# Out projection issued in code order, with next weights split inside the last column tile; adaLN-side weight pairs loaded two K tiles ahead

## The chip, the cores and the metric

The kernel runs on one core of one Trainium2 chip. The metric is the device time of one execution in microseconds (us). The core has a matrix engine (TensorE, PE in the rows; its weight loads are PEld), VectorE (DVE), ScalarE (ACT), GpSimd (POOL) and SyncE (SP). In this kernel every DMA is issued by SP, from one queue, in order. An issue can wait for a semaphore, and then everything behind it on SP waits too.

## The reference, cut to what matters

One layer of a hybrid decoder on 2048 prompt tokens and 8 single-token samples, model width 2048, all in fp32:

```python
shift, scale, gate = split(silu(c) @ w_c + b_c, 3)          # adaLN
h    = rmsnorm(x, g_pre) * (1 + scale) + shift
proj = h @ w_in                                             # u_a, v_a, z_a, x_b, z_b
y_a  = u_a * mix(layernorm(v_a)) * silu(z_a)                # gated MLP, chunks of 128 tokens
y_b  = glu(S5(x_b)) * silu(z_b)                             # diagonal state space model
o    = concat(y_a, y_b) @ w_out
out  = x + gate * rmsnorm(o, g_post)
```

## The kernel before, in words

**Precision.** Each fp32 factor is split in two rounded parts, hi and lo, and each product is three matmuls: hi by hi, hi by lo, lo by hi (`mm3`, L97 to L99). A weight tile comes by DMA as a raw tile `wraw` of 128x1024 (0.524 MB, L108); its two halves ("pieces") are split by ACT (`whi`, L90) and then by DVE or POOL (`wlo`, L85). `lo_engs` says which engine makes the lo of the next piece: DVE and POOL in turn, and in block 3 and behind it DVE, DVE, DVE, POOL. Each tag of split weights has 5 buffers (NW), the raw tiles have 3.

**Startup.** It is written in manual order. SP loads the 16 x tiles, small constants, and the adaLN weights (`wraw<-in_wss`, 64 tiles, 8 in flight). DVE builds a small selector `sel` from the identity (L230, L232) and adds up the squares of x (L342). Then a loop over 16 K tiles multiplies 6 column tiles of w_in with h while it makes the adaLN vectors that the next K tile needs: 4 matmul groups `ada` (L275), a copy `t<-ada` by DVE (L279), a selection `adat` by PE (L286), and a scale of x. The weights of the 6 column tiles come as three pairs (`wraw<-in_win`, tag wraw2, 2 buffers), one set for each group of 4 K tiles; before, a pair is asked for in the first two K tiles of the group that uses it.

**Middle.** Input projection, gated MLP and S5 of four blocks of 512 tokens (phase 1). Tile's scheduler orders these by its own cost estimates. In the S5 part small matrices are copied out of PSUM, `sc` and half of `kf` by DVE.

**Out projection.** `phase3(b)` does 512 tokens of block b (blocks 0 to 2): first a K loop over 16 K tiles with 4 column tiles side by side, then the column tiles n = 4 to 15 one after the other, each with 16 K tiles of 3 matmuls. Block 3 has 264 tokens in this form and 6 tiles side by side. `phase3_rows` does the last 256 tokens the other way round: y is stationary, 32 weight tiles (`wraw<-in_woutr`, called W(i) here) of 2 pieces each feed 12 matmuls each, W(i+4) is asked for while step i runs.

**Finish.** The output of a block is finished in 16 steps while the next block (for block 3, the rows stage) multiplies. The generator `final` loads the residual `xres`, makes the rms factor `oR`, and in each step n:

```python
            V.tensor_mul(o, o, R[:, 0:nn])
            (V if n % 2 else G).tensor_tensor(o, o, x, op=ALU.add)
            SP.dma_start(self.O["yT"][...], o)
            yield 1
```

These are L1154, L1155 and L1156 (with L1145 the load of `xres`); in the changed kernel they are L1156, L1157, L1158 and L1147. `finish_some(n)` takes n steps. O(n) below is the output DMA of step n. In the kernel before, Tile's scheduler also orders all of the out projection: what stands in the code is not the order on an engine.

Of the kernel before, what the change touches and what calls it, by code (L numbers as in the profile page):

```python
# [11 lines left out]
F32 = mybir.dt.float32  # L12
# [11 lines left out]
NB = 4  # L24
# [3 lines left out]
G = 64  # L28
GC = 16
P = 64  # L30
KT = D // 128
# [11 lines left out]
NHL = 32  # L43
NT = 6
NW = 5
OB = 20
LAG = 6
NR_ = 8
XR0 = 41
# [13 lines left out]
class Builder:  # L63
# [155 lines left out]
    def constants1(self):  # L219
        c = self.cp  # L220
        def load(name, shape):
            t = c.tile(shape, F32, name="c_" + name)
            self.SP.dma_start(t, self.I[name])
            return t
        self.ident = load("ident", [128, 128])
        self.bcT = load("bcT", [128, 48])
        self.gpre = load("gpre", [128, KT])
        self.gpost = load("gpost", [128, KT])
        self.sel = c.tile([128, 9], F32, name="sel")
        self.V.tensor_add(self.sel, self.ident[:, 0:9], self.ident[:, 32:41])  # L230
        for i in (64, 96):
            self.V.tensor_add(self.sel, self.sel, self.ident[:, i : i + 9])  # L232

    def constants2(self):
        I, SP, V, S, T = self.I, self.SP, self.V, self.S, self.T
# [510 lines left out]
    def s5_mats(self, pp, i):  # L746


        V, SP, I, T, G, S = self.V, self.SP, self.I, self.T, self.G, self.S
        X = G  # L750
        NQ = 2
# [4 lines left out]
        b = tl([128, 2, NQ, GC], "sb", 2)  # L756
# [39 lines left out]
                k = (ri * NQ + q) * 32  # L796
                T.matmul(pc[:, k : k + 32], cp[:, q, ri, :], wg[:, q, :], start=True, stop=True)
        c = tl([128, 2, NQ, 32], "sc")
        V.tensor_copy(c.rearrange("p r q c -> p (r q c)"), pc[:, 0 : 2 * NQ * 32])
        dw = tl([32, NQ, 32], "dw")  # L800
        mul(dw, wg, dc[:, :, None].to_broadcast([32, NQ, 32]))
        yield
# [47 lines left out]
                T.matmul(pk[g * 32 : g * 32 + 32, 0:128], bd[:, ri, q].rearrange("p g c -> p (g c)"),  # L850
                         Fm[:, ri, q, jh * 4 : jh * 4 + 4, :].rearrange("p j c -> p (j c)"), start=ri == 0, stop=ri == 1)
        for g, q, jh in quarters:
            (S.copy if jh else V.tensor_copy)(kf[:, q, jh * 4 : jh * 4 + 4, :].rearrange("p j c -> p (j c)"), pk[g * 32 : g * 32 + 32, 0:128])
# [238 lines left out]
    def phase3(self, b, ws, y):  # L1092

        V, G, SP = self.V, self.G, self.SP
        rs = ranges(b) if b < NB - 1 else ranges(b)[1:]
        c0 = rs[0][0]
        nn = rs[-1][0] + rs[-1][1] - c0
        ng = 4 if b < NB - 1 else 6
        ssq = self.xp.tile([128, TB + ND], F32, tag="ssq", bufs=2, name=self.nm("ossq"))
        kw = [{}, self.wkw]  # L1100
        ws = ws or [self.wgroup(0, 0, ng, *kw)]
        acc = [[self.ps.tile([128, 512], F32, tag="acc" if g < 4 else "aux", bufs=4, name=self.nm("acc"))] for g in range(ng)]
        os_ = []
        for k in range(KT):
            while len(y) < min(KT, k + 6):
                y.append(self.yload(b, len(y)))
            if k in (11, 13, 15):
                self.finish_some(1)
            if k % 4 == 0 and k < KT - 4:
                ws.append(self.wgroup(0, k // 4 + 1, ng, *(kw[::-1] if k // 4 % 2 == 0 else kw)))  # L1110
            for g in range(ng):
                self.kstep(acc[g], ws[k // 4][g], k, y[k], rs, k == 0, k == KT - 1)
        ynext = []
        w = self.wcol(self.I["wout"][ng])
        for g in range(ng):
            self.finish_some(1)
            os_.append(self.ev_o(b, g, acc[g], rs, ssq, G))
        for n in range(ng, 16):
            ac = [self.ps.tile([128, 512], F32, tag="acc", bufs=4, name=self.nm("acc")) for _ in rs]
            nxt = []  # L1120
            for k in range(KT):
                if k % 8 == 0 and n < 15:
                    nxt += self.wsplit(self.whalf(self.I["wout"][n + 1], k // 8), **(self.wkw if k else {}))
                self.kstep(ac, w, k, y[k], rs, k == 0, k == KT - 1)
                if k == 13:
                    self.run_later()
                if n == 15 and b < NB - 1 and k >= 4 and k % 2 == 0:
                    ynext.append(self.yload(b + 1, len(ynext)))
            self.finish_some(1 if n < 15 or b == NB - 1 else 16)
            if b == NB - 1 and n % 2 == 0 and 6 <= n < 14:  # L1130
                self.gg_rows((n - 6) // 2)
            os_.append(self.ev_o(b, n, ac, rs, ssq, G))
            w = nxt
        self.finish_some(16)
        self.finish = self.final(ssq, nn, os_, b * TB + c0, b * TB)
        return y if b == NB - 1 else ynext

    def final(self, ssq, nn, os_, t0, out0):

# [19 lines left out]
    def gg_rows(self, f):  # L1159

        dg = self.tile_()[:, 0:512]
        for j in range(4):
            self.S.activation(dg[:, j * 128 : j * 128 + 128], self.ident, AF.Identity, scale=self.GG[:, f * 4 + j, 0:1])
        def turn():
            po = self.ps.tile([128, 512], F32, tag="aux", bufs=4, name=self.nm("ggr"))
            self.T.matmul(po, self.ones, dg, start=True, stop=True)
            t = self.tile_()[:, 0:512]
            self.S.copy(t, po)
            self.ggr.append(t)
        self.later.append(turn)  # L1170

    def phase3_rows(self, b, y):
# [3 lines left out]
        src = lambda i: self.I["woutr"][i // 8][:, i % 8 * 2 : i % 8 * 2 + 2, :].rearrange("p k m -> p (k m)")  # L1176
        kws = [{}, self.wkw]
        ws = {i: self.wsplit(src(i), **kws[i % 2]) for i in range(4)}
        os_, xs = {}, {}
        mm = T.matmul  # L1180
        def final(c):
# [18 lines left out]
        for f in range(4):  # L1200
# [3 lines left out]
            for k in range(KT + lag):  # L1204
# [19 lines left out]
                            final(c)  # L1224
                if k < KT and k % 2:
                    if i + 4 < 32:
                        ws[i + 4] = self.wsplit(src(i + 4), **kws[i % 2])
# [9 lines left out]
    def startup(self, st, NG, ntl):  # L1237
# [6 lines left out]
                raws[i] = self.wraw(I["wss"][i // 4][:, i % 4 * 4 : i % 4 * 4 + 4, :].rearrange("p k m -> p (k m)"), st, "sraw", NR_)  # L1244
        ws = [[] for _ in range(NG)]
        def wraw(g, kq):
            pair[g, kq] = self.wraw(self.wpair(I["win"], ntl[1][g], kq), st, "wraw2", 2)
        def wsplit(g, kq):
            a, b = self.wpieces(pair.pop((g, kq)), pool=st, tags=("swh", "swl"), bufs=NG + 2, engs=(V, G))
            ws[g].append(a)  # L1250
# [2 lines left out]
        self.constants1()  # L1253
        for i in range(NR_):
            raw(i)
        wraw(0, 0)
        wraw(2, 0)
        ssq = self.tile_()
        for k in range(KT):
            self.stat_add(st, xs[k], ssq, k, TB, V)  # L1260
        R = self.R[0]
        def ada(ps, i):
            self.ada_mm(ps, raws.pop(i), i % 4)
            raw(i + NR_)
# [8 lines left out]
        sb = self.ada_copy(ps)  # L1273
        self.hscale(xs[0], R, 0)
        wsplit(0, 0)
        wraw(4, 0)
        self.ada_ss2(0, sb)
        self.h = [self.hmake(xs[0], 0, 0)]
        wsplit(2, 0)
# [7 lines left out]
        for s in range(2, KT + 2):  # L1287
# [6 lines left out]
            for q in range(NG):  # L1294
# [11 lines left out]
                if q == 2 and prev is not None:  # L1306
                    self.h.append(self.hmake(xs[s - 1], 0, s - 1))
                if s < KT:
                    if s % 4 == 0 and q in (0, 2):
                        wraw(q, s // 4)  # L1310
                    if s % 4 == 1 and q == 3:
                        wraw(4, s // 4)
                    if (s % 4, q) in ((0, 3), (1, 2), (1, 4)):
                        wsplit(0 if q == 3 else q, s // 4)
            if s == KT:
# [4 lines left out]
    def build(self):  # L1320
# [127 lines left out]
        cm_x, self.xp = self.pool("x3")  # L1448
        self.finish = None
        self.wkw = {"pool": self.xp, "tags": ("w3h", "w3l"), "bufs": 5}  # L1450
        for b in range(NB):
            if b == NB - 1:
                self.lo_engs = [V, V, V, G]
                self.ggr = []
            y = self.phase3(b, [ws0] if b == 0 else None, y0 if b == 0 else y)
        self.phase3_rows(NB - 1, y)
        self.close(cm_x)
        for cm in reversed(cms[1:]):
            self.close(cm)
# [71 lines left out]
```

## Time and profile before

| what | value |
|---|---|
| time, median of 3 runs | 2974.43 us (2973.07 to 2980.24) |
| the profiled execution | 2969.24 us |
| its span, first to last instruction | 2967.4 us |
| PE busy | 2846.7 us, 96% of the span |
| DVE, ACT, POOL busy | 1590.0, 1059.7, 1046.0 us |
| mean granted TensorE clock | 0.987 of full speed |
| moved by DMA | 581.14 MB, 196 GB/s over the span |

PE has work nearly all of the time, so the time is the sum of the matmuls and of the places where PE stops. A matmul counts as busy until its modelled end; the number of matmuls in a stretch says more than the busy share. A queue of SP is written SPq. A row of a timeline gives the start, the length, the engine, the line and the operation, and in brackets how long the engine had been idle before it and what ended that.

### The profile page before, as it was taken

To read this page: it belongs to the slowest core of one execution; us is meant where nothing else is said; L and a number is where in the kernel's file an instruction comes from. 1 tells how busy PE (TensorE), PEld (TensorE's weight loads), DVE (VectorE), ACT (ScalarE), POOL (GpSimd) and SP (SyncE) were. 2 spreads that over 40 slices of the span, in tenths; PEclk is the share of its full clock that TensorE was granted. 3 is DMA by queue.
4 is the path that set the end of the run, shared out by engine and by line. 5 is a ranking of instruction groups with operands and counts; after the bars stand their busy time and mean duration, and the time that the engine had idled before them with its cause. 6 is when DMAs were issued, how large, how long until landed. Compare 5 with 4: busy or idle time off the path is not lost.

```text
span 2967.4 us, 44344 instructions
## 1 busy us (share of the span) xinstructions
PE 2846.7 (96%) x15804; PEld 2387.4 (80%) x15804; DVE 1590.0 (54%) x3026; ACT 1059.7 (36%) x1960; POOL 1046.0 (35%) x971
## 2 busy tenths in 40 slices
PE   5899899999999999999999999999999999999896
PEld 3567677777999999988888888888888878878785
DVE  4347946648543646466546745583641361543755
ACT  3224433433333232333334332433243423434442
POOL 0107735364242232323232223222324353352433
PEclk9999999999999999999999999999999999999998
DMA  8777898997887373856576566646573463564666
GB/s 299 270 201 217 237 258 236 258 270 221 194 205 214 105 232 119 251 163 189 166 215 195 161 193 185 209 132 215 162 217 110 117 206 121 142 213 128 202 199 206
DMA packets 456560, 581.14 MB, mean 196 GB/s; under 512 B 216594, under 2 KB 303122, under 8 KB 456338
## 3 DMA queue, kind: packets, MB, share of 16 engines
q1 hardware_dynamic: 456338, 578.32, 65.3%
q8 instruction: 124, 2.03, 0.3%
q14 instruction: 98, 0.79, 0.1%
HBM read 466.87 MB, written 102.66 MB: 192 GB/s over the span
## 4 chain that ended last, share of the span: by engine, by line
PE 57%; DVE 8%; DMA 3%; issue 2%; ACT 1%; SPq 0%; POOL 0%; DVEq 0%; ACTq 0%; POOLq 0%
PE acc L99 17%; PE acc L97 16%; PE acc L98 16%; DVE Ub L898 2%; DVE o L1154 1%; DVE wlo L85 1%; DMA x<-in_xT 1%; DMA wraw<-in_wout 1%; PE mix L530 1%; PE acc L1214 1%; PE acc L1215 1%; PE acc L1216 1%; DMA wraw<-in_woutr 1%; PE pg L979 1%; DVE sct L908 1%
## 5 line engine op out<-in xcount | busy, mean ns | idle before, releaser
L97 PE MATMUL acc<-hi,whi 128*128 128x512 f32 (+2 forms) x3200 | 1131.4, 355 | 4.0 <-DVE x L374 2.2
L98 PE MATMUL acc<-lo,whi 128*128 128x512 f32 (+2 forms) x3200 | 1122.3, 351 | 2.4 <-DVE lo L85 2.1
L99 PE MATMUL acc<-hi,wlo 128*128 128x512 f32 (+2 forms) x3200 | 1122.0, 351 | 1.9 <-DVE wlo L85 1.6
L85 DVE TENSOR_TENSOR wlo<-wraw,whi 128x512 fp32r<-128x512 f32 x628 | 518.9, 835 | 882.4 <-ACT whi L90 858.5
L90 ACT CAST whi<-wraw 128x512 fp32r<-128x512 f32 x960 | 581.4, 621 | 1142.7 <-PE acc L98 791.0
L85 POOL TENSOR_TENSOR wlo<-wraw,whi 128x512 fp32r<-128x512 f32 x332 | 459.8, 1387 | 1131.8 <-ACT whi L90 1027.3
L97 PEld LDWEIGHTS acc<-hi,whi 128*128 128x128 f32 x3200 | 603.2, 189 | 100.7 <-issue 23.4
L99 PEld LDWEIGHTS acc<-hi,wlo 128*128 128x128 f32 x3200 | 603.6, 189 | 90.7 <-DVE wlo L85 4.7
L98 PEld LDWEIGHTS acc<-lo,whi 128*128 128x128 f32 x3200 | 604.6, 189 | 80.2 <-DVE lo L85 3.9
L99 PE MATMUL acc<-yhi,wlo 128*128 128x512 f32 (+1 forms) x1024 | 379.6, 372 | 16.7 <-DVE wlo L85 15.2
L97 PE MATMUL acc<-yhi,whi 128*128 128x512 f32 (+1 forms) x1024 | 378.6, 370 | 6.4 <-ACT whi L90 3.6
L98 PE MATMUL acc<-ylo,whi 128*128 128x512 f32 (+1 forms) x1024 | 378.3, 370 | 0.0
L99 PEld LDWEIGHTS acc<-yhi,wlo 128*128 128x128 f32 x1024 | 195.3, 191 | 54.5 <-DVE wlo L85 18.0
L97 PEld LDWEIGHTS acc<-yhi,whi 128*128 128x128 f32 x1024 | 195.6, 191 | 42.5 <-ACT whi L90 4.1
L98 PEld LDWEIGHTS acc<-ylo,whi 128*128 128x128 f32 x1024 | 195.4, 191 | 34.0
L898 DVE SCALAR_TENSOR_TENSOR Ub<-Ub,apow 128x128 f32<-128x128 f32 (+6 forms) x384 | 143.3, 440 | 2.5 <-ACT Ub L885 2.2
L987 POOL TENSOR_TENSOR sg<-sg,zbl 128x264 f32<-128x264 f32 x64 | 54.7, 855 | 191.6 <-DVE sg L986 127.8
L1076 POOL TENSOR_TENSOR ossq<-ossq,osq 128x512 f32<-128x512 f32 (+1 forms) x60 | 81.8, 1363 | 47.8 <-ACT osq L1069 47.0
L369 ACT ACTIVATE hi<-x,shiftT 128x512 fp32r<-128x512 f32 x96 | 68.4, 724 | 82.1 <-DVE x L368 78.8
L368 DVE SCALAR_TENSOR_TENSOR x<-x,GT,R 128x512 f32<-128x512 f32 x96 | 82.2, 872 | 23.9 <-DMA x<-in_xT 23.7
L90 ACT CAST hh<-hr 128x264 fp32r<-128x264 f32 x64 | 26.4, 414 | 191.4 <-DMA hr<-Ub 107.3
L342 POOL TENSOR_TENSOR ssq<-ssq,t 128x512 f32<-128x512 f32 (+1 forms) x45 | 60.9, 1353 | 72.7 <-ACT t L341 71.8
(287 smaller groups left out, 2798.5 us busy)
## 6 DMA issues: line engine op xcount, KB each, us to landing
wraw<-in_win SPq DMA_DIRECT2D x320, 512.0 KB
wraw<-in_wout SPq DMA_DIRECT2D x128, 512.0 KB
xr<-XB SPq DMA_DIRECT2D x128, 272.0 KB
x<-in_xT SPq DMA_DIRECT2D x128, 256.0 KB
wraw<-in_wss SPq DMA_DIRECT2D x64, 512.0 KB
XB<-t SPq DMA_DIRECT2D x64, 256.0 KB
wraw<-in_wgt SPq DMA_DIRECT2D x32, 512.0 KB
MQ<-qh SPq DMA_DIRECT2D x128, 128.0 KB
```

The lines of the kernel that those rows point to most:

```text
L85: eng.tensor_tensor(out, a, b, op=ALU.subtract)
L90: self.S.copy(hi, raw)
L97: mm(acc, whi, xhi, start=start, stop=False)
L98: mm(acc, whi, xlo, start=False, stop=False)
L99: mm(acc, wlo, xhi, start=False, stop=stop)
L342: add_eng.tensor_tensor(ssq[:, 0:n], ssq[:, 0:n], sq[:, 0:n], op=ALU.add)
L368: V.scalar_tensor_tensor(xt, xt, self.GT[:, k, 0:1], R[:, 0:TB], op0=ALU.mult, op1=ALU.mult)
L369: S.activation(hi[:, 0:TB], xt, AF.Identity, bias=self.shiftT[:, k, 0:1])
L530: T.matmul(pm[:, c * 128 : c * 128 + 128], self.vtok[:, c, hs], self.wsT[:, h, :], start=True, stop=True)
L898: V.scalar_tensor_tensor(o, i, f, o, op0=ALU.mult, op1=ALU.add)
L987: self.G.tensor_tensor(sg, sg, zb, op=ALU.mult)
L1076: eng.tensor_tensor(ssq[:, 0:nn], ssq[:, 0:nn], sq[:, 0:nn], op=ALU.add)
```

## The change

- `phase3` for all blocks and `phase3_rows` stand in one `with tc.manual_schedule()`: each engine gets these instructions in the order of the code.
- In the last column tile (n = 15) the first weight pairs of the next block (or the first two W of the rows stage) are loaded and split between the K steps. The finish steps of the K loop stand behind the matmuls of K tiles 11, 13 and 15 and not ahead of them.
- Startup: wraw2 has 3 buffers; the third first pair is asked for with the first two; a group's pairs are asked for in the third K tile of the group before it. The adds that build `sel` stand behind the adds of the squares.
- S5: the copies `sc` and `kf` go from DVE to ACT.
- Buffers: 19 tiles for o and not 20; the broadcast gate rows `ggr` have a tag of their own.

```diff
-        self.sel = c.tile([128, 9], F32, name="sel")          # constants1, ahead of the squares
-        self.V.tensor_add(self.sel, self.ident[:, 0:9], self.ident[:, 32:41])
...
-        V.tensor_copy(c.rearrange("p r q c -> p (r q c)"), pc[:, 0 : 2 * NQ * 32])
+        S.copy(c.rearrange("p r q c -> p (r q c)"), pc[:, 0 : 2 * NQ * 32])
...
-            (S.copy if jh else V.tensor_copy)(kf[:, q, jh * 4 : jh * 4 + 4, :]...)
+            S.copy(kf[:, q, jh * 4 : jh * 4 + 4, :]...)
...                                                             # phase3, K loop
-            if k in (11, 13, 15):
-                self.finish_some(1)
             if k % 4 == 0 and k < KT - 4:
                 ws.append(self.wgroup(0, k // 4 + 1, ng, ...))
             for g in range(ng):
                 self.kstep(acc[g], ws[k // 4][g], k, y[k], rs, k == 0, k == KT - 1)
+            if k in (11, 13, 15):
+                self.finish_some(1)
...                                                             # phase3, column tiles
-                if n == 15 and b < NB - 1 and k >= 4 and k % 2 == 0:
-                    ynext.append(self.yload(b + 1, len(ynext)))
+                if n == 15 and b < NB - 1:
+                    if k >= 4 and k % 2 == 0:
+                        ynext.append(self.yload(b + 1, len(ynext)))
+                    if k in (1, 9) or (k == 13 and b == NB - 2):
+                        g = len(wnext)
+                        wnext.extend(self.wsplit(self.wpair(self.I["wout"], g, 0), **kw[g // 4]))
+                elif n == 15 and k in (1, 9):
+                    wnext.append(self.rows_w(len(wnext)))
...                                                             # startup
-            pair[g, kq] = self.wraw(self.wpair(I["win"], ntl[1][g], kq), st, "wraw2", 2)
+            pair[g, kq] = self.wraw(self.wpair(I["win"], ntl[1][g], kq), st, "wraw2", 3)
...
-        wraw(0, 0)
-        wraw(2, 0)
+        for g in (0, 2, 4):
+            wraw(g, 0)
         ssq = self.tile_()
         for k in range(KT):
             self.stat_add(st, xs[k], ssq, k, TB, V)
         R = self.R[0]
+        self.sel = self.cp.tile([128, 9], F32, name="sel")
+        V.tensor_add(self.sel, self.ident[:, 0:9], self.ident[:, 32:41])
...
-                    if s % 4 == 0 and q in (0, 2):
-                        wraw(q, s // 4)
-                    if s % 4 == 1 and q == 3:
-                        wraw(4, s // 4)
+                    if s % 4 == 2 and s < KT - 4 and q % 2 == 0:
+                        wraw(q, s // 4 + 1)
...                                                             # build
-        for b in range(NB):
-            ...
-            y = self.phase3(b, [ws0] if b == 0 else None, y0 if b == 0 else y)
-        self.phase3_rows(NB - 1, y)
+        with tc.manual_schedule():
+            for b in range(NB - 1):
+                y, ws = self.phase3(b, ws, y)
+            self.lo_engs = [V, V, V, G]
+            self.ggr = []
+            y, ws = self.phase3(NB - 1, ws, y)
+            self.phase3_rows(NB - 1, y, ws)
```

**Startup, SP.** Before, at the beginning of the loop: the adaLN tiles (`in_wss`) run on, and a pair (`in_win`) comes two K tiles later, apart from the next.

```order
L108 DMA wraw_448<-in_wss 128x1024
L108 DMA wraw_454<-in_wss 128x1024
L108 DMA wraw_474<-in_wss 128x1024
L108 DMA wraw_480<-in_wss 128x1024
L108 DMA wraw_504<-in_wss 128x1024
L108 DMA wraw_510<-in_wss 128x1024
L108 DMA wraw_530<-in_wss 128x1024
L108 DMA wraw_536<-in_wss 128x1024
L108 DMA wraw_545<-in_win 128x2x512
```

The same stretch in the changed kernel:

```order
L108 DMA wraw_433<-in_win 128x2x512
L108 DMA wraw_450<-in_wss 128x1024
L108 DMA wraw_456<-in_wss 128x1024
L108 DMA wraw_463<-in_win 128x2x512
L108 DMA wraw_471<-in_win 128x2x512
L108 DMA wraw_480<-in_wss 128x1024
```

The three pairs of the second group stand ahead of 8, 8 and 12 adaLN tiles that they stood behind.

**From block 0 to block 1, SP.** Before: four weight tiles of 128x1024, for the column tiles 4 and 5 of block 1, stand ahead of the first output O(0) of block 0.

```order
L108 DMA wraw_23840<-in_wout 128x1024
L108 DMA wraw_23850<-in_wout 128x1024
L108 DMA wraw_23899<-in_wout 128x1024
L108 DMA wraw_23933<-in_wout 128x1024
L1047 DMA t_24769<-YA_0_97 128x512
L1047 DMA t_24781<-YA_1_98 128x512
L1047 DMA t_24793<-YA_2_99 128x512
L1047 DMA t_24805<-YA_3_100 128x512
L1047 DMA t_24817<-YA_4_101 128x512
L1047 DMA t_24829<-YA_5_102 128x512
L1156 DMA out_yT<-o_22538 128x512
```

The changed kernel:

```order
L1158 DMA out_yT<-o_22540 128x512
L1147 DMA xres_23808<-in_xT 128x512
L1158 DMA out_yT<-o_22543 128x512
L1147 DMA xres_23837<-in_xT 128x512
L1158 DMA out_yT<-o_22548 128x512
L108 DMA wraw_23842<-in_wout 128x1024
L108 DMA wraw_23852<-in_wout 128x1024
L1147 DMA xres_23862<-in_xT 128x512
L1158 DMA out_yT<-o_22553 128x512
```

The weights of column tile 4 stand behind O(0), O(1) and O(2); those of tile 5 stand further down, behind O(6).

**Rows stage, SP and DVE.** Before, SP, the last of 19 W in a row and the first outputs of block 3 behind them:

```order
L108 DMA wraw_28022<-in_woutr 128x1024
L108 DMA wraw_28049<-in_woutr 128x1024
L108 DMA wraw_28076<-in_woutr 128x1024
L1156 DMA out_yT<-o_26789 128x264
L1145 DMA xres_27895<-in_xT 128x264
L1145 DMA xres_27924<-in_xT 128x264
L1156 DMA out_yT<-o_26808 128x264
L1156 DMA out_yT<-o_26789 128x264
```

The changed kernel, SP, the same outputs (W(11) is `wraw_27916`):

```order
L1147 DMA xres_27897<-in_xT 128x264
L1158 DMA out_yT<-o_26791 128x264
L108 DMA wraw_27916<-in_woutr 128x1024
L1147 DMA xres_27926<-in_xT 128x264
L1158 DMA out_yT<-o_26810 128x264
L108 DMA wraw_27943<-in_woutr 128x1024
L1147 DMA xres_27953<-in_xT 128x264
L1158 DMA out_yT<-o_26810 128x264
L108 DMA wraw_27970<-in_woutr 128x1024
```

And DVE there:

```order
L85 TENSOR_TENSOR wlo_27923<-wraw_27916,whi_27922 128x512
L1156 TENSOR_TENSOR o_26810<-o_26810,oR_27834 128x264
L85 TENSOR_TENSOR wlo_27950<-wraw_27943,whi_27949 128x512
L1156 TENSOR_TENSOR o_26810<-o_26810,oR_27834 128x264
L1157 TENSOR_TENSOR o_26810<-o_26810,xres_27862 128x264
L85 TENSOR_TENSOR wlo_27973<-wraw_27970,whi_27972 128x512
L85 TENSOR_TENSOR wlo_27977<-wraw_27970,whi_27976 128x512
L1156 TENSOR_TENSOR o_26831<-o_26831,oR_27834 128x264
```

SP has one W between two outputs, and so on for all 16 outputs; DVE has the lo of that W ahead of the multiplication for the next output. (In block 3 two column tiles share one buffer `o_...`, so each name comes twice.)

## Rows read from the trace of the kernel before

**Rows 1.** Waits of PE, 0 to 240 us: total, times, longest.

```profile
PE adat L286 <- DVE t L279: 20.9, 7, 6.3
```

**Rows 2.** Timeline of the startup loop, 71 to 83 us.

```profile
71.42 0.38 SPq L108 DMA_DIRECT2D wraw<-in_win  x1
...
80.38 0.62 ACT L90 CAST whi<-wraw 128x512 fp32r<-128x512 f32 x1 [7.46 <-DMA wraw<-in_win]
...
82.12 1.02 PE L286 MATMUL adat<-sel,t 128*128 128x9 f32 x4 [6.35 <-DVE t L279]
```

**Rows 3.** Timeline of PE: four of the 15 adat in the loop.

```profile
46.34 0.61 PE L286 MATMUL adat<-sel,t 128*128 128x9 f32 x4 [2.35 <-DVE t L279]
...
91.34 0.51 PE L286 MATMUL adat<-sel,t 128*128 128x9 f32 x4
98.36 0.51 PE L286 MATMUL adat<-sel,t 128*128 128x9 f32 x4
...
172.34 0.51 PE L286 MATMUL adat<-sel,t 128*128 128x9 f32 x4
```

**Rows 4.** Windows: length, busy (count) by engine, PEclk, DMA share, GB/s.

```profile
100.00:110.00 10.00, 10.00 (x78) 6.17 (x67) 4.71 (x8) 4.42 (x8) 1.50 (x2) 1.00 1.02 373
117.40:124.20 6.80, 6.42 (x28) 4.02 (x29) 2.70 (x5) 1.44 (x2) 1.13 (x1) 0.50 0.27 75
2300.00:2400.00 100.00, 100.00 (x433) 81.02 (x432) 37.15 (x44) 39.10 (x60) 29.73 (x22) 1.00 0.42 123
2820.00:2840.00 20.00, 18.99 (x153) 18.79 (x154) 12.16 (x17) 11.90 (x25) 7.93 (x7) 1.00 0.74 236
```

**Rows 5.** Timeline of DVE and ACT before the loop.

```profile
15.87 0.17 DVE L230 TENSOR_TENSOR sel<-c_ident 128x9 f32<-128x9 f32 x1 [11.24 <-DMA c_ident<-in_ident]
...
16.36 11.82 DVE L342 TENSOR_TENSOR t<-t,t 128x512 f32<-128x512 f32 x15
...
29.13 0.62 ACT L90 CAST whi<-wraw 128x512 fp32r<-128x512 f32 x1 [3.46 <-DMA wraw<-in_win]
```

**Rows 6.** Waits of PE, 2150 us to the end.

```profile
PE acc L99 <- DVE wlo L85: 15.2, 5, 5.3
```

**Rows 7.** Waits of SP's queue, 2180 us to the end.

```profile
SPq L108 <- DVE wlo L85: 413.8, 120, 9.5
...
SPq L1156 <- POOL o L1155: 19.1, 14, 4.7
```

**Rows 8.** Timeline of DVE, POOL and PE between block 1 and block 2.

```profile
2391.50 0.69 DVE L160 TENSOR_SCALAR t<-ssum 128x512 f32<-128x512 f32 x1 [7.88 <-PE ssum L159]
...
2401.04 19.02 DVE L1154 TENSOR_TENSOR o<-o,oR 128x512 f32<-128x512 f32 x15
...
2401.81 1.68 POOL L1155 TENSOR_TENSOR o<-o,xres 128x512 f32<-128x512 f32 x1 [8.56 <-DVE o L1154]
...
2421.32 0.74 PE L99 MATMUL acc<-yhi,wlo 128*128 128x512 f32 x1 [4.57 <-DVE wlo L85]
```

**Rows 9.** Timeline of the rows stage.

```profile
2854.20 0.33 SPq L108 DMA_DIRECT2D wraw<-in_woutr  x1
...
2857.75 1.14 ACT L90 CAST whi<-wraw 128x512 fp32r<-128x512 f32 x2 [1.47 <-DMA wraw<-in_woutr]
2858.41 1.29 DVE L85 TENSOR_TENSOR wlo<-wraw,whi 128x512 fp32r<-128x512 f32 x2 [1.36 <-ACT whi L90]
...
2861.91 1.36 DVE L85 TENSOR_TENSOR wlo<-wraw,whi 128x512 fp32r<-128x512 f32 x1 [2.21 <-ACT whi L90]
...
2894.65 1.86 POOL L1155 TENSOR_TENSOR o<-o,xres 128x264 f32<-128x264 f32 x2
2898.44 0.42 DVE L1155 TENSOR_TENSOR o<-o,xres 128x264 f32<-128x264 f32 x1
...
2909.31 0.38 SPq L108 DMA_DIRECT2D wraw<-in_woutr  x1
...
2915.42 0.80 PE L1214 MATMUL acc<-whi,yhi 128*128 128x512 f32 x1 [8.42 <-ACT whi L90]
```

More of the change, by code (lines that the diff above doesn't have):

```diff
@@ L45 @@
 NW = 5
-OB = 20
+OB = 19
 LAG = 6
@@ L228, in constants1 @@
         self.gpost = load("gpost", [128, KT])
-        self.sel = c.tile([128, 9], F32, name="sel")
-        self.V.tensor_add(self.sel, self.ident[:, 0:9], self.ident[:, 32:41])
-        for i in (64, 96):
-            self.V.tensor_add(self.sel, self.sel, self.ident[:, i : i + 9])
     def constants2(self):
@@ L852, in s5_mats @@
         for g, q, jh in quarters:
-            (S.copy if jh else V.tensor_copy)(kf[:, q, jh * 4 : jh * 4 + 4, :].rearrange("p j c -> p (j c)"), pk[g * 32 : g * 32 + 32, 0:128])
+            S.copy(kf[:, q, jh * 4 : jh * 4 + 4, :].rearrange("p j c -> p (j c)"), pk[g * 32 : g * 32 + 32, 0:128])
         V.tensor_add(kf[:, :, 0, :], kf[:, :, 0, :], dw)
@@ L1100, in phase3 @@
         kw = [{}, self.wkw]
-        ws = ws or [self.wgroup(0, 0, ng, *kw)]
+        ws = [ws]
         acc = [[self.ps.tile([128, 512], F32, tag="acc" if g < 4 else "aux", bufs=4, name=self.nm("acc"))] for g in range(ng)]
@@ L1112, in phase3 @@
                 self.kstep(acc[g], ws[k // 4][g], k, y[k], rs, k == 0, k == KT - 1)
-        ynext = []
+            if k in (11, 13, 15):
+                self.finish_some(1)
+        ynext, wnext = [], []
         w = self.wcol(self.I["wout"][ng])
@@ L1135, in phase3 @@
         self.finish = self.final(ssq, nn, os_, b * TB + c0, b * TB)
-        return y if b == NB - 1 else ynext
+        return (y if b == NB - 1 else ynext), wnext
     def final(self, ssq, nn, os_, t0, out0):
@@ L1166, in turn @@
             self.T.matmul(po, self.ones, dg, start=True, stop=True)
-            t = self.tile_()[:, 0:512]
+            t = self.xp.tile([128, 512], F32, tag="ggr", bufs=4, name=self.nm("ggt"))
             self.S.copy(t, po)
@@ L1170, in gg_rows, with rows_w, phase3_rows @@
         self.later.append(turn)
-    def phase3_rows(self, b, y):
+    def rows_w(self, i):
+        return self.wsplit(self.I["woutr"][i // 8][:, i % 8 * 2 : i % 8 * 2 + 2, :].rearrange("p k m -> p (k m)"), **(self.wkw if i % 2 else {}))
+    def phase3_rows(self, b, y, ws):
         V, G, S, T, SP = self.V, self.G, self.S, self.T, self.SP
         ssq = self.sp_.tile([128, 2, 4], F32, name="ssqr")
-        src = lambda i: self.I["woutr"][i // 8][:, i % 8 * 2 : i % 8 * 2 + 2, :].rearrange("p k m -> p (k m)")
-        kws = [{}, self.wkw]
-        ws = {i: self.wsplit(src(i), **kws[i % 2]) for i in range(4)}
+        ws = dict(enumerate(ws))
+        for i in range(len(ws), 4):
+            ws[i] = self.rows_w(i)
         os_, xs = {}, {}
@@ L1226, in phase3_rows @@
                     if i + 4 < 32:
-                        ws[i + 4] = self.wsplit(src(i + 4), **kws[i % 2])
+                        ws[i + 4] = self.rows_w(i + 4)
                     if f or k >= 13:
@@ L1261, in startup @@
         R = self.R[0]
+        self.sel = self.cp.tile([128, 9], F32, name="sel")
+        V.tensor_add(self.sel, self.ident[:, 0:9], self.ident[:, 32:41])
+        for i in (64, 96):
+            V.tensor_add(self.sel, self.sel, self.ident[:, i : i + 9])
         def ada(ps, i):
@@ L1450, in build @@
         self.wkw = {"pool": self.xp, "tags": ("w3h", "w3l"), "bufs": 5}
-        for b in range(NB):
-            if b == NB - 1:
-                self.lo_engs = [V, V, V, G]
-                self.ggr = []
-            y = self.phase3(b, [ws0] if b == 0 else None, y0 if b == 0 else y)
-        self.phase3_rows(NB - 1, y)
+        y, ws = y0, ws0
+        with tc.manual_schedule():
[5 more added lines that the diff above has]
+            self.phase3_rows(NB - 1, y, ws)
         self.close(cm_x)
```

1 line of the change is left out of this document (removed).

## The prediction

> **What bounds the kernel now.** PE is busy for 96% of the span, so I first read the waits of PE, in three stretches, to see what it loses. In the startup it waits 20.9 us in 7 places for one thing, the copy ahead of `adat` [rows 1]. In the out projection it waits 15.2 us in 5 places for a `wlo` of DVE [rows 6], and 8.42 us once for a `whi` near the end [rows 9]. The middle, 2000 us long, is not touched but for a few copies. Then I read timelines around these waits.
>
> In the startup the reader is to see that the copy is only the last link: the weight pair was issued at 71.42, its `whi` began at 80.38, ACT and DVE worked in the order of the code, and so the copy behind that `wlo` came late and PE stood for 6.35 us [rows 2]. After such a stop PE's granted clock is 0.50 for 6.8 us, which is the 1.2 GHz level [rows 4].
>
> In the out projection the reader is to see who stands in line. SP waits 413.8 us in 120 places for a `wlo` before it can issue the next weights: it runs as far ahead as the buffers allow, and this is harmless. But it also waits for the adds of POOL before an output [rows 7]. Whatever stands behind such an output on SP waits as well.
>
> **Startup.** Undisturbed, a K tile takes 98.36 - 91.34 = 7.02 us. From the first to the last of the 15 `adat` it is 172.34 - 46.34 = 126.0 us, against 14 x 7.02 = 98.3 [rows 3]. So the loop loses 27.7 us: the waits, and the half clock behind them. In the changed kernel each pair is issued two K tiles (some 14 us) earlier; 8.96 us from issue to `whi` [rows 2] are then covered. I count all 27.7.
>
> DMA has to keep up: a K tile needs 4 adaLN tiles and three quarters of a pair, 4.75 x 0.524 MB = 2.49 MB in 7.02 us, or 355 GB/s. Windows of 10 us show 373 GB/s [rows 4]. The row leaves 5%. If the rate were short of it, the pairs would push the adaLN tiles late and half of the gain would stay: -14 us is my lower bound.
>
> The Trainium skill speaks against this term: DMA: Bandwidth & Descriptors, Specifications, gives about 358 GB/s as the HBM share of one core. By that a K tile could not be under 6.96 us, so the loop's 98.3 us would still fit, but nothing could be caught up; by the row, nearly 5 us of it are to spare. The row decides here, since it exceeds the figure.
>
> Ahead of the loop, the first add of the squares waits behind `sel`, which waits for the identity until 15.87; only then do 15 adds run, 0.79 us each, until 28.2 [rows 5]. With `sel` behind them they follow the x tiles as these land and end some 10 us earlier. The first `whi` starts at 29.13, when its pair has landed [rows 5], so that soon becomes the limit; between that and the first `adat` of the loop lay 46.34 - 29.13 = 17 us, of which the rms factor was the late part. I take -9.5, bounds -5 and -11. Startup together: -37, bounds -19 and -39.
>
> **S5 copies.** The two kinds of copies go from DVE to ACT, some hundred short ones in a stretch where DVE is busier than ACT and where PE waits for neither. I take 0, bounds -8 and +8 (the order of the scheduled part shifts with them).
>
> **Out projection.** The part in code order makes a loop that the scheduler's order did not have. On SP: W, `xres`, O(n), next W. O(n) waits for the add of step n; the add waits for the multiplication; that stands on DVE behind the `wlo` of the W just issued; and that waits for the W to land. So the next W is not even asked for until this one has landed and gone through. The prefetch distance of four W is of no use while the loop runs.
>
> *Rows stage.* One turn: issue to `whi` 2857.75 - 2854.20 = 3.55 us; `whi` start to the end of the second `wlo` 2.0 us when both are DVE's, about 2.5 when POOL has one (1.14 for both `whi`, then 1.36 for a `wlo` beside POOL's); multiplication 0.4; add 0.42 on DVE or 0.93 on POOL (1.86 for two) [rows 9]; two issues on SP of 0.33 to 0.38 each with what lies between them, 0.4. The step with both `wlo` on DVE has the add on POOL and the other one on DVE, so the sum is 7.3 either way; I take 7.25. PE needs 12 matmuls for a W, and 433 of them take 100 us [rows 4]: 12 x 0.231 = 2.78 us. There are 16 outputs, from step 6 on. W(11) is the first behind an output. The squares of block 3 are summed and `oR` is made just there, so I put its issue 9.75 us behind the middle of step 6, and W(26) 15 turns later, at 9.75 + 108.75 = 118.5. Its first matmul is at 118.5 + 3.55 + 0.7 = 122.8. Without a wait it would be at 19.5 x 2.78 = 54.2. The loss is 68.6 us, bounds 55 (a turn of 6.4) and 75. Before, the same outputs came in one burst and delayed one W, asked for at 2909.31, which cost 8.42 us [rows 9], with the half clock and smaller stops behind block 3 some 16 in all. Difference +52, bounds +39 and +59.
>
> *Block 3.* Its column tiles take 48 x 0.131 = 6.3 us [rows 4], while a turn of the same loop has two weight tiles: the rows-stage turn and 1.5 us for the second load (0.524 MB at 357 GB/s), some 8.8 us. Over 7 column tiles that is 17.5; the first two tiles, whose weights stand behind O(2) and O(8), wait 10 each, and the K loop 7 (6 tiles side by side with 5 buffers of each tag). Sum 45. Before, the waits and half clock of that block sum to 21.5. Difference +23, bounds +8 and +35.
>
> *From block 0 to 1 and 1 to 2.* The weights of column tile 4 now stand behind O(2). After K tile 11 the rms chain takes 2401.04 - 2391.50 = 9.5 us [rows 8], a multiplication 0.7 and an add on POOL 1.7, and O(0) goes; O(1) and O(2) follow, so the weights are asked for some 14.9 us after the end of K tile 11. The tile can be split and used 4.3 us later, at 19.2; PE wants it after four K tiles of 2.78 us, at 11.1. That is a stop of 8.1, with 3 for tile 5 behind O(6) and 2 of half clock 13. Before, DVE's 15 multiplications in a row held a `wlo` and cost 4.57 [rows 8] and half clock, 6.3. Difference +7 each, +14, bounds +4 and +24. The later column tiles take 11.1 us, a turn takes about 9.5: no wait there.
>
> The early loads inside the last column tile and the steps moved behind a K tile change nothing by themselves: PE does not wait for the first weights of a block in the trace before, and I count them at 0; if the scheduler had not already hoisted them, they would save one load of 3.55 us at each of three borders.
>
> **Sum.** -37 + 0 + 14 + 23 + 52 = +52 us. From the profiled 2969.2 us this gives 3021, a ratio of 1.0175; on the median of 2974.4 it is **3026 us**. The low bounds together give -39 - 8 + 4 + 8 + 39 = +4, the high ones -19 + 8 + 24 + 35 + 59 = +107; not all ends meet at once.
>
> **The rivals.**
>
> 1. *The loop does not bind (faster).* It needs that DVE and POOL reach the adds before W is through, or that the outputs do not hold SP. The SP waits for POOL's adds [rows 7] speak against the second, the order on DVE against the first. If a turn were at or below 2.78 us, the stops of before would go as well: -37, and between nothing and the 50 us that the out projection loses before (12.6 at two borders, 21.5, 16), so 2887 to 2937 us; I would name 2920. The loop costs something from a turn of 2.78 us on. It decides the sign from a turn of 3.7 us on if the borders and block 3 cost what I count (the rows stage then loses 68.6 - 15 x 3.55 = 15, as before), and from 6.2 on if they cost nothing.
> 2. *The loop binds only in the rows stage and with short turns (about the same).* With turns of 5.25 us the rows stage loses 38.6, or +22; with half of block 3's term (+12) and nothing at the borders the sum is -3, 2971 us on the median.
> 3. *DMA bounds the startup as well.* The pairs come early but the adaLN tiles late; then -19 in place of -37, and 3044 us. For it speaks 355 against 373 GB/s, a small margin [rows 4].
> 4. *The out projection is as now.* If the code's order came close to the scheduler's, only the startup's -37 would be left, 2937 us. The shown orders on SP speak against it.
>
> **How the numbers follow.** The forecast with its loop 0.70, rival 3 (still slower) 0.09, rival 2 0.06, rivals 1 and 4 together 0.15. What a measurement here can tell from no change is 0.3%, 9 us. Slower by more than that: 0.79; within: 0.06; faster: 0.15. The range leaves out rivals 1 and 4 and the far ends: 2975 to 3070 us.
>
> **What would show it.** Startup: the `adat` 7.02 us apart from the first to the last, that wait gone from PE's list, the first loop `adat` near 36. Rows stage: PE waits for `whi` or `wlo` about 4.5 us in each of some 15 W, the clock at its lower level, some 33 matmuls in 20 us in place of 87; SP's waits for `o` many times those of before. Block borders: one stop of 8 us ahead of column tile 4. The prediction is wrong if SP issues two W while one output is pending, if the first `adat` stays near 46, or if the turns in the rows stage are under 5 us.

## The result, and the profile after

The changed kernel takes 3082.89 us (median, 3081.76 to 3086.61) against 2973.75 of the kernel before in the same comparison: a ratio of 1.0365, 95% interval 1.0347 to 1.0383. The forecast was 3026, with a range to 3070. So it is slower, as forecast, but by 109 us and not by 52. One label ahead was off by one: in the order shown, W(11) is `wraw_27887` and `wraw_27916` is W(12); no number hangs on it.

Where the time went, by stages. A stage starts with its first matmul; the lengths are in us, and the last line is the span. PE's matmuls are the same ones in both kernels, so a stage that is longer has stops, or a lower clock.

| stage | before | after | difference | forecast |
|---|---|---|---|---|
| startup, to the last `adat` of the loop | 172.3 | 136.1 | -36.3 | -37 |
| middle, to block 0's out projection | 2009.9 | 2009.9 | 0.0 | 0 |
| block 0 | 178.0 | 179.3 | +1.3 | 0 |
| block 1 | 184.9 | 202.2 | +17.3 | +7 |
| block 2 | 184.6 | 202.1 | +17.5 | +7 |
| block 3, 264 tokens | 120.8 | 169.9 | +49.1 | +23 |
| rows stage | 102.9 | 168.5 | +65.6 | +52 |
| end | 13.9 | 12.9 | -1.0 | |
| span | 2967.4 | 3080.9 | +113.5 | +52 |

The same stages after, in the windows of the profile (length, busy time and count of PE, PEld, DVE, ACT, POOL, then PE's granted clock, DMA share, GB/s):

```profile
0.00:136.00 136.00, 113.43 (x846) 71.63 (x847) 61.42 (x130) 45.78 (x72) 17.67 (x16) 0.97 0.93 338
...
2325.30:2527.50 202.20, 184.44 (x771) 145.45 (x770) 92.70 (x85) 66.72 (x113) 80.97 (x55) 0.97 0.48 146
...
2729.50:2899.50 170.00, 120.53 (x780) 113.26 (x779) 82.07 (x117) 63.09 (x133) 47.42 (x39) 0.82 0.55 163
2899.50:3068.00 168.50, 121.96 (x388) 85.84 (x386) 60.28 (x104) 40.33 (x78) 26.04 (x24) 0.79 0.40 126
```

The reader is to see that in the two stages that grew most, block 3 and the rows stage, no engine is near full (PE 121 and 122 us of 170 and 168.5), the DMA share is 0.55 and 0.40, and the granted clock is 0.82 and 0.79: everything waits for something.

**Startup, after.** Rows of `adat` in PE's timeline, to be read beside [rows 3]:

```profile
35.26 1.02 PE L282 MATMUL adat<-sel,t 128*128 128x9 f32 x4 [1.06 <-DVE t L275]
44.81 0.51 PE L282 MATMUL adat<-sel,t 128*128 128x9 f32 x4
51.83 0.51 PE L282 MATMUL adat<-sel,t 128*128 128x9 f32 x4
...
136.06 0.51 PE L282 MATMUL adat<-sel,t 128*128 128x9 f32 x4
```

The `adat` stand 7.02 us apart from 44.81 on; the first is 11.1 us earlier than before, the loop from the first to the last takes 100.8 us and not 126.0. DMA moves 338 GB/s over the whole stage.

**What PE and SP wait for, after.** The waits of PE over the whole span, beside [rows 6]:

```profile
PE acc L1220 <- ACT whi L90: 42.7, 16, 6.7
PE acc L97 <- ACT whi L90: 30.9, 10, 7.6
PE acc L97 <- ACT o L1067: 25.5, 4, 12.4
...
PE acc L97 <- DVE o L1069: 15.2, 1, 15.2
```

The weights' `whi` is what PE waits for most, and that is ACT's cast of a tile that has just landed. The waits of SP's queue from 2146 us on, beside [rows 7]:

```profile
SPq L1158 <- POOL o L1157: 243.6, 32, 26.3
SPq L108 <- DVE wlo L85: 218.3, 55, 19.9
SPq L1158 <- DVE o L1157: 172.0, 20, 10.8
```

Before, the outputs waited 19.1 us in all for POOL's adds [rows 7] and as long for DVE's, in a row of the same view:

```profile
SPq L1156 <- DVE o L1155: 19.1, 5, 8.8
```

Now the outputs hold SP for 243.6 + 172.0 us, and the wait for free weight buffers, the harmless one, has fallen from 413.8 to 218.3: SP no longer runs ahead.

**One turn of the loop in the rows stage,** in the timelines of SP, ACT, DVE and POOL, beside [rows 9]:

```profile
2934.95 0.43 SPq L108 DMA_DIRECT2D wraw<-in_woutr  x1
...
2938.74 1.14 ACT L90 CAST whi<-wraw 128x512 fp32r<-128x512 f32 x2 [6.46 <-DMA wraw<-in_woutr]
...
2939.39 1.29 DVE L85 TENSOR_TENSOR wlo<-wraw,whi 128x512 fp32r<-128x512 f32 x2 [4.87 <-ACT whi L90]
2940.61 0.43 DVE L1156 TENSOR_TENSOR o<-o,oR 128x264 f32<-128x264 f32 x1
...
2941.11 0.75 POOL L1157 TENSOR_TENSOR o<-o,xres 128x264 f32<-128x264 f32 x1 [7.94 <-DVE o L1156]
...
2941.89 0.34 SPq L1158 DMA_DIRECT2D out_yT<-o  x1
2942.64 0.33 SPq L108 DMA_DIRECT2D wraw<-in_woutr  x1
```

From request to request 7.69 us here; in the mean of 12 turns, by the first matmul of a W from 2939.42 to 3027.97, 7.4. Each of these instructions waits for the one shown above it, and the brackets show that ACT, DVE and POOL stood idle for 5 to 8 us ahead of it: one weight tile is under way at a time, and these steps do not overlap.

**At a border,** SP, ACT and PE from block 0 to block 1, beside [rows 8]:

```profile
2372.52 0.34 SPq L1158 DMA_DIRECT2D out_yT<-o  x1
2372.92 0.91 SPq L108 DMA_DIRECT2D wraw<-in_wout  x2
...
2379.35 2.40 ACT L90 CAST whi<-wraw 128x512 fp32r<-128x512 f32 x4 [29.22 <-DMA wraw<-in_wout]
...
2382.14 0.68 ACT L1067 ACTIVATE o<-acc,GG 128x512 f32<-128x512 f32 x1
...
2382.88 0.80 PE L97 MATMUL acc<-yhi,whi 128*128 128x512 f32 x1 [12.43 <-ACT o L1067]
```

The list of waits blames ACT's copy out of PSUM. The reader should go one link further back: that copy stands on ACT behind the four casts of the weights of column tile 4, and these wait for a load that SP asked for at 2372.92, behind O(2).

### The profile page after: what moved, and what is told of

The parts are those of the page before. It is cut to its first block, busy times and chain, and to the rows that moved or that the text cites. A ratio compares the mean times of both kernels' runs of the same rounds, so it can differ in the third digit from the quotient of the medians.

```text
span 3080.9 us, 44269 instructions
## 1 busy us (share of the span) xinstructions
PE 2892.4 (94%) x15804; PEld 2405.9 (78%) x15804; DVE 1626.8 (53%) x2976; ACT 1059.2 (34%) x2008; POOL 1049.5 (34%) x973
## 4 chain that ended last, share of the span: by engine, by line
PE 66%; DMA 11%; DVE 10%; issue 6%; POOL 4%; ACT 2%; SPq 2%; DVEq 0%; POOLq 0%; ACTq 0%
PE acc L97 20%; PE acc L99 19%; PE acc L98 19%; DMA wraw<-in_wout 5%; DMA x<-in_xT 2%; DVE wlo L85 2%; DMA wraw<-in_woutr 1%; PE ada L271 1%; ACT whi L90 1%; POOL wlo L85 1%; DVE lo L366 1%; POOL o L1157 1%; DVE Ub L894 1%; DVE o L1156 1%; DVE x L364 1%
## 5 line engine op out<-in xcount | busy, mean ns | idle before, releaser
L85 DVE TENSOR_TENSOR wlo<-wraw,whi 128x512 fp32r<-128x512 f32 x626 | 568.2, 919 | 1004.0 <-ACT whi L90 993.1
L90 ACT CAST whi<-wraw 128x512 fp32r<-128x512 f32 x960 | 572.7, 619 | 1183.7 <-PE acc L98 638.0
L85 POOL TENSOR_TENSOR wlo<-wraw,whi 128x512 fp32r<-128x512 f32 x334 | 472.3, 1419 | 1084.3 <-ACT whi L90 1024.0
L97 PE MATMUL acc<-yhi,whi 128*128 128x512 f32 (+1 forms) x1024 | 389.5, 380 | 71.8 <-ACT whi L90 30.9
L99 PE MATMUL acc<-yhi,wlo 128*128 128x512 f32 (+1 forms) x1024 | 387.8, 379 | 8.9 <-POOL wlo L85 8.0
L98 PE MATMUL acc<-ylo,whi 128*128 128x512 f32 (+1 forms) x1024 | 384.7, 376 | 0.0
L97 PEld LDWEIGHTS acc<-yhi,whi 128*128 128x128 f32 x1024 | 201.9, 197 | 112.6 <-ACT whi L90 36.0
L98 PEld LDWEIGHTS acc<-ylo,whi 128*128 128x128 f32 x1024 | 201.6, 197 | 34.6 <-issue 1.0
L1220 PE MATMUL acc<-whi,yhi 128*128 128x512 f32 x128 | 62.0, 485 | 42.7 <-ACT whi L90 42.7
```

The source lines that it names most:

```text
L85: eng.tensor_tensor(out, a, b, op=ALU.subtract)
L90: self.S.copy(hi, raw)
L97: mm(acc, whi, xhi, start=start, stop=False)
L98: mm(acc, whi, xlo, start=False, stop=False)
L99: mm(acc, wlo, xhi, start=False, stop=stop)
L1220: mm(acc[c], yh, wh, start=kc == 0, stop=False)
```

## The experiments

The theory (A) is the loop of the prediction: through the outputs on SP, a weight request waits for the weights before it. Rivals: (B) it is the code order on DVE, ACT and PE that costs, not SP; (C) the transfers are too slow.

**e1_startup and e2_outproj: one half of the change each.** The first has, on the kernel before, the hunks for startup and the S5 copies, the second the rest.

> The kernel before with the startup part and the S5 copies of the change, the out projection ordered by the scheduler as before. In the trace of the changed kernel the last adat of the loop comes 36.3 us earlier and the middle is as long as before. Both theories: 2974 - 36 = 2938 us (2930 to 2946). A rival on the startup (the gain is only shifted work and is given back by the scheduler's order behind it): within 9 us of 2974.

> The kernel before with the out projection in code order alone, startup and copies as before. If the two parts add up: 3083 + 36 = 3119 us (3110 to 3128). If the earlier startup had moved something that the out projection then paid for: less than 3105.

Measured: 2934.89 us, ratio 0.9865 (0.9850 to 0.9880), and 3121.02 us, ratio 1.0488 (1.0470 to 1.0506). Both as expected: -41 and +145 sum to +104, against +109 for the whole, a difference that the intervals cover. The startup's gain is not given back.

**e8_sel and e9_pairs: two parts of the startup alone** (the `sel` hunk; the four hunks on `wraw`).

> The kernel before with only the adds of sel moved behind the squares. My term for the head was -9.5 us (-5 to -11), and the trace of the changed kernel has its first adat of the loop 11.1 us earlier, with the third pair moved as well. Theory: 2974 - 10 = 2964 us. Rival (the pairs that are asked for late hold the loop anyway, so the head's gain is lost in the loop): within 4 us of 2974.

> The kernel before with only the weight pairs asked for earlier and three buffers for them. My term for the loop was -27.7 us and the changed kernel's loop is 25.2 us shorter. Theory: 2974 - 26 = 2948 us (2944 to 2952). Rival (DMA is full, the adaLN tiles come late instead): 2955 to 2965 us.

Measured: 2969.69 us, ratio 0.9977 (0.9966 to 0.9988), and 2944.23 us, ratio 0.9895 (0.9877 to 0.9913). The first lies between theory and rival. The first two rows of `adat` in PE's timeline of e8_sel say why; below them are the last `adat` of the loop in e8_sel and in e9_pairs:

```profile
28.32 1.02 PE L282 MATMUL adat<-sel,t 128*128 128x9 f32 x4 [0.55 <-DVE t L275]
40.03 1.02 PE L282 MATMUL adat<-sel,t 128*128 128x9 f32 x4 [4.95 <-DVE t L275]
...
167.62 0.51 PE L282 MATMUL adat<-sel,t 128*128 128x9 f32 x4
...
142.45 0.51 PE L286 MATMUL adat<-sel,t 128*128 128x9 f32 x4
```

The adaLN vectors of the first K tile come 9.5 us earlier than before (28.32; before 37.80), but the next `adat` then stops for 4.95 us, since the third pair is still asked for late; 6.3 us are left there, and 4.7 at the end of the loop (167.62; before 172.34). The pairs alone gave 31 us, the most that was expected, and 29.9 at the end of the loop. Together the two hunks give 36.3 there, so most of the gain is the pairs'; that the two are worth more together than apart is not shown, since the times do not resolve it.

**e3_defer3 and e7_defer1: outputs later on SP, nothing else.**

```diff
+        outs = []
...
-            SP.dma_start(self.O["yT"][n * 128 : n * 128 + 128, out0 : out0 + nn], o)
+            outs.append((n, o))
+            while len(outs) > (3 if n < 15 else 0):      # e7_defer1: 1 and not 3
+                m, om = outs.pop(0)
+                SP.dma_start(self.O["yT"][m * 128 : m * 128 + 128, out0 : out0 + nn], om)
             yield 1
```

> The changed kernel with each output DMA issued three finish steps later, so that on SP three more weight requests stand ahead of it; the multiplications and adds stay where they are in the order of DVE and POOL. Theory A (the loop through SP: a weight request waits for an output that hangs on the weight before): a turn of the rows stage falls from 7.3 to under 2.8 us, rows from 168 to about 100 us, block 3 from 170 to about 125, each of the two borders a few us less, so 2930 to 2970 us. Rival B (the code order on DVE, ACT and PE costs the time, the queue of SP does not matter): within 15 us of 3083. Rival C (transfers are too slow): within 15 us of 3083, DMA share near 1 in the rows stage.

> The changed kernel with each output DMA one finish step later (three in the run before, none in the change). Theory A: two weights are on their way in each turn of 7.3 us, so a W every 3.65 us against the 2.78 that PE needs: rows stage between 116 us (three later) and 168 us (none), near 125; blocks 3 in between too; the whole 2985 to 3020 us. Rival B (some other effect of the three steps, not the number of weights under way): 2976 as with three, or 3083 as with none.

Measured: 2976.09 us with three steps (ratio to the kernel before 1.0005, 0.9995 to 1.0015), 2983.18 with one (1.0031, 1.0017 to 1.0045). The order on DVE, ACT, POOL and PE is that of the changed kernel, and yet 107 us are gone, of the 145 that the out projection costs by itself in e2_outproj: for these, B and C fall. (That the time is back at that of the kernel before is chance: the startup still gives its 41, and the out projection still loses about as much.) The rows stage takes 116.2 us with three steps, 120.5 with one, 168.5 with none, in the order that four loads in a turn, two, and one would give (I had put it near 100 with three steps and near 125 with one); block 3 takes 133.7 with three steps, where I had about 125. The numbers missed my ranges by 6 and by 2 us, on opposite sides.

```profile
2843.30:2959.50 116.20, 99.28 (x388) 73.14 (x386) 60.95 (x104) 40.10 (x78) 26.51 (x24) 0.94 0.59 184
```

But the stop at a border stayed in e3_defer3, 9.92 us ahead of column tile 4. So something else held its weights.

**e4_earlyw: the weights of column tile 4 ahead of the finish steps.**

```diff
+            if k == 11 and b < NB - 1:
+                w = self.wsplit(self.whalf(self.I["wout"][ng], 0)) + self.wsplit(self.whalf(self.I["wout"][ng], 1))
             if k in (11, 13, 15):
                 self.finish_some(1)
```

> The changed kernel with the weights of column tile 4 of blocks 0 to 2 requested and split behind K tile 11, ahead of the finish steps (in the other tag of split weights, which is free there); block 3 and the rows stage unchanged. Theory A (the stop of 12.4 us at a border is the late request): the two stops go, with the half clock behind them 13 to 17 us each, so 3050 to 3058 us. Rival B (the stop is PSUM, set free by ACT only behind the casts of these weights): the casts are early too, so the same; but if it is the order of the finish steps themselves, no more than 3 us each, 3077 us and over.

Measured: 3062.15 us, 21 less than the changed kernel, where 25 to 33 less were expected. The stop of 12.43 us behind ACT's copy is gone. As this run moves the request and the casts together, it cannot tell a late request from the order on ACT; e10_late_xres below can. Column tile 5, whose weights still stand behind O(6), now stops for 5.25 us, where it stopped for 1.57 in the changed kernel:

```profile
2390.51 0.80 PE L97 MATMUL acc<-yhi,whi 128*128 128x512 f32 x1 [5.25 <-ACT whi L90]
```

**e6_early_finish: the finish begun with the next K loop,** outputs three steps later: the split of the squares at K tile 0 ahead of the first weights, then one step behind every odd K tile; in the rows stage from step 2.

> Outputs three steps later, and the finish of a block begun at the start of the next K loop (the squares are split ahead of the first weights, then a step in every second K tile) and not at K tile 11; in the rows stage from step 2 on. Theory A (what is left at the borders and in block 3 is the rms chain of 9.5 us and the first outputs falling just ahead of the weights of the first single column tile): the stops of 10 us at two borders and of 13 us and 8 us in block 3 shrink to a few us, 2976 - 30 = 2945 us (2925 to 2958). Rival (these stops are PSUM set free late by ACT, or the two tags of weight buffers): no change, 2968 to 2980.

Measured: 3008.23 us, ratio 1.0105 (1.0087 to 1.0122), worse than e3_defer3; expectation and rival both missed. The stop ahead of column tile 4 is still 9.09 us. SP's timeline there:

```profile
2375.72 0.33 SPq L1164 DMA_DIRECT2D xres<-in_xT  x1
2376.09 0.43 SPq L1182 DMA_DIRECT2D out_yT<-o  x1
2376.62 0.90 SPq L108 DMA_DIRECT2D wraw<-in_wout  x2
```

The weights stand right behind a residual load, and that load waits too: it needs the buffer of an earlier residual, which is free only after the add. The waits of SP's queue in this run, from 2144 us on, show how long:

```profile
SPq L1164 <- POOL o L1178: 168.1, 22, 20.0
```

This I had overlooked: there are two kinds of DMA on SP that hang on an add. There are new stops inside the K loops of blocks 1 and 2 (1.5 to 3.3 us each), and block 3 is 13 us longer than in e3_defer3; the cause of these was not looked into.

**e10_late_xres, e12_late_xres_only and e11_late_xres_earlyw: residual loads two steps later,** with outputs three steps later, with outputs at their place, and with both and the early weights of e4_earlyw.

```diff
-            if n < 13:
+            if 2 <= n < 15:
                 load()
```

> Outputs three steps later, finish steps back at K tiles 11, 13 and 15, and the residual loads two steps later (step n loads the residual of step n + 1, from step 2 on). In the run with early finish the stops ahead of column tile 4 stayed, and its SP timeline shows the weights behind a residual load that waits for an add. Theory A, widened (any DMA on SP that waits for an add holds the weights, residual loads as well as outputs): at a border the weights are asked for ahead of the end of the K loop, the stop falls from 10 to about 4 us (four casts and one copy out of PSUM on ACT remain), in block 3 from 13.4 and 7.8 to about 5 and 1, so 2976 - 25 = 2951 us (2940 to 2960). Rival (the stops are ACT's order and the PSUM tiles): 2970 to 2980 us.

> The changed kernel with the residual loads two steps later and the outputs at their place (the fourth corner beside none, outputs later, both). Theory A: the outputs alone still close the loop, so the rows stage keeps its turns of 7.3 us and the borders their stops, since O(0) to O(2) stand ahead of the weights: 3083 less no more than 10 us, 3073 to 3085. Rival (the residual loads were the holder all along, and with outputs later they only came free): near 2926, or half way, 3000 to 3030.

> The run e10_late_xres with the weights of column tile 4 of blocks 0 to 2 also requested and split behind K tile 11 ahead of the finish steps. Theory A: what is left of the stop at the two borders goes, 4 us and some half clock each: 8 to 12 us under e10_late_xres, near 2940, about what the startup part alone gives (2935). Rival (the casts ahead of the finish delay the rms chain and the loss only moves to column tile 5, as 5.3 us did in e4_earlyw): within 4 us of e10_late_xres.

Measured: e10_late_xres 2926.44 us, ratio 0.9835 (0.9819 to 0.9851); e12_late_xres_only 3090.20, ratio 1.0387 (1.0370 to 1.0404), 5 us over its range; e11_late_xres_earlyw 2921.87, ratio 0.9819 (0.9802 to 0.9835). So four corners: neither 3083, residuals later alone 3090 (whether that is slower than neither is open, since the two intervals overlap), outputs later alone 2976, both 2926. Outputs close the loop; once they are out of the way, the residual loads are the next to hold SP. The windows of blocks 1 and 3 and of the rows stage in e10_late_xres:

```profile
2323.30:2507.30 184.00, 180.56 (x771) 145.53 (x770) 92.79 (x85) 66.09 (x113) 80.31 (x55) 0.99 0.52 160
...
2691.20:2813.30 122.10, 106.29 (x780) 101.97 (x779) 83.58 (x117) 63.33 (x133) 48.67 (x39) 0.93 0.76 226
2813.30:2908.90 95.60, 91.85 (x388) 72.57 (x386) 62.08 (x104) 40.51 (x78) 27.12 (x24) 0.98 0.71 223
```

The granted clock is back at 0.93 or above in these stages. What PE still waits for there, from 2130 us on:

```profile
PE acc L97 <- DVE o L1069: 6.2, 1, 6.2
PE acc L99 <- POOL wlo L85: 5.5, 3, 2.5
PE ssum L158 <- ACT sqh L90: 4.6, 2, 4.3
PE acc L97 <- ACT whi L90: 3.4, 1, 3.4
```

Blocks 1 to 3 are within 1.3 us of the scheduler's, and the rows stage is 7.3 us shorter than before, at 95.6. The two stops at a border are 0.9 and 2.5 us where the first alone was 12.43; block 3 keeps 6.2, 4.3 and 3.4. The border settles what e4_earlyw left open. The casts stand ahead of the copy on ACT as in the changed kernel, and only the request is early:

```profile
2343.26 1.96 SPq L108 DMA_DIRECT2D wraw<-in_wout  x2
...
2366.18 2.02 ACT L90 CAST whi<-wraw 128x512 fp32r<-128x512 f32 x3 [16.52 <-PE acc L98]
...
2368.59 0.68 ACT L1067 ACTIVATE o<-acc,GG 128x512 f32<-128x512 f32 x1
...
2369.32 0.50 PE L97 MATMUL acc<-yhi,whi 128*128 128x512 f32 x1 [0.91 <-ACT o L1067]
```

So it was the late request that made the stop long. The kernel of e10_late_xres beats both: 50 us under the one before, 156 under the change, and 8 us under e1_startup, which has the scheduler's order (the two intervals just touch, so that this lead is not firm). Between e10_late_xres and e11_late_xres_earlyw (5 us, intervals overlap, 8 to 12 us expected) the runs do not decide.

## Why the prediction was wrong in size

*Startup, -37:* right, -36.3, and by stretches too: loop -25.2 for -27.7, head -11.1 for -9.5. By edits the split is another: the `sel` hunk alone gives 4.7 us at the end of the loop, the pairs alone 29.9. DMA did not bound the loop, though it had little to spare: in the changed kernel it moved 355 GB/s there, what the forecast asked for, at a share of 0.99, and PE did not stop once:

```profile
44.80:115.00 70.20, 70.20 (x541) 45.05 (x540) 28.22 (x57) 21.61 (x34) 10.15 (x7) 1.00 0.99 355
```

The figure of the Trainium skill that I had weighed against it (DMA: Bandwidth & Descriptors, Specifications, about 358 GB/s as the limit of one core) lies above this rate, so no run here puts it to the test as a lasting rate; the 373 GB/s of [rows 4] are one window of 10 us, and the 5% to spare that I read from it are not shown. Rival 3 is out: the loop kept its 7.02 us.

*S5 copies, 0:* right; the middle is 2009.9 us in both.

*Rows stage, +52, measured +65.6:* the mechanism was right and the turn nearly so: 7.25 forecast, 7.4 measured, and the first W behind an output was asked for at 2927.43, 9.9 us behind the middle of step 6, where I had 9.75. The first matmul of W(26) comes 128.6 us behind that middle and not 122.8. Some 2 us of this are the longer turn; the rest is at the end, where a residual `xr` load of the rows stage is issued between the output and the weights and the last two turns are 8.6 and 9.6 us. Behind it PE has 84 matmuls left, 12 more than my sum had, since in the last column group of the code one half of the tokens runs six K tiles late; that is 2.8 us. These 84 take 21.8 us and not 19.4, with a granted clock of 0.50 at first. And before, 2 us less were lost than I had counted. One sign came out otherwise: PE waits 2.7 us for each W (42.7 in 16 places) and not 4.5. The granted clock is not at its lower level throughout, and the slower matmuls fill a part of each turn:

```profile
2931.00:3050.00 119.00, 72.83 (x179) 46.44 (x177) 33.46 (x52) 21.75 (x43) 16.71 (x16) 0.70 0.38 118
```

*Block 3, +23, measured +49.1:* the step that failed is the price of a turn with two weight tiles, 8.8 us. SP's timeline of the changed kernel has two such requests one turn apart:

```profile
2800.10 0.88 SPq L108 DMA_DIRECT2D wraw<-in_wout  x2
...
2811.19 0.87 SPq L108 DMA_DIRECT2D wraw<-in_wout  x2
```

And ACT's casts of the first two, in its timeline:

```profile
2805.14 1.14 ACT L90 CAST whi<-wraw 128x512 fp32r<-128x512 f32 x2 [7.10 <-DMA wraw<-in_wout]
2806.44 1.14 ACT L90 CAST whi<-wraw 128x512 fp32r<-128x512 f32 x2 [0.16 <-DMA wraw<-in_wout]
```

The turn is 11.1 us. The first of two loads asked for together takes 5.04 us to its `whi`; I had taken 3.55, the time of a load asked for alone [rows 9]. That is 1.5 of the 2.3 us. Most of the rest is a second thing that I had overlooked. The outputs finished in this stage are those of block 2, 512 tokens wide, and I had taken the multiplication (0.4) and the add (0.42 on DVE) of the rows stage, which finishes outputs of 264. DVE in the same turn:

```profile
2808.89 0.68 DVE L1156 TENSOR_TENSOR o<-o,oR 128x512 f32<-128x512 f32 x1
2809.60 1.12 DVE L1157 TENSOR_TENSOR o<-o,xres 128x512 f32<-128x512 f32 x1
```

Seven turns of 11.1 in place of 8.8 are 16 of the 26 us that were missing; the stops ahead of the first two column tiles (15.19 and 7.56 us, forecast 10 each) are 3. The other 7 were not taken apart; the granted clock is 0.82 in this stage. (A small misreading beside it: the row that I read as 6.3 us for a column tile [rows 4] has PE busy for 18.99 of its 20 us, which gives 6.0.)

*Borders, +14, measured +34.8:* the same wrong price, twice. The weights were asked for 14.2 us behind the end of K tile 11 (forecast 14.9), but the load took 6.43 us (two weights, and outputs and residuals beside them), and then PE waited for four casts and a copy out of PSUM on ACT, 3.5 us from the first cast to PE's start, where I had 0.7 for the split. The stop is 12.43 us and not 8.1, which is 4.3 of the 10.3 us missing there. That ACT frees the PSUM tiles only behind the casts was in the code and not in my sum. Five later column tiles of block 1 wait 0.56 to 0.63 us each for a `wlo` of POOL, 3 us that I had at nothing. The rest was not taken apart; part of it is the clock behind the stop, 0.58 from 2383 to 2390 us.

Each of the three terms came out above its own upper bound: 65.6 against 59, 49.1 against 35, 34.8 against 24. The price of one load asked for alone stands in block 3 and at the borders alike, so these two missed together. Rivals 1, 2 and 4 are out as well: the turns are 7.4 us, and block 3 and the borders lose time too.

## What to carry to other kernels

Where one in-order queue issues both loads and stores, look at what each store and each load waits for: a load put behind a store that hangs on the previous load is a prefetch of depth one, however many buffers there are. Moving the stores (and every other DMA that waits on late work) a few steps down the queue was worth 156 us here, while the order on the other engines stayed as it was. Price a load in the company in which it is issued: here the first of two asked for together took 5.04 us to its cast, and one alone 3.55.

## What the runs showed that I had not expected

Of two 0.524 MB loads issued back to back the first took 5.04 us to its cast and the second 1.3 us more, while one alone took 3.55 to 3.79 us. The outputs issued just ahead of the two are also wider here (512 tokens and not 264), and no run tells the two reasons apart. And one change of place on a queue can hide what the next is worth: residuals later gave nothing alone (3090 against 3083), and 50 us once the outputs were later too.
